# Moving two token-major product steps to the front of a layer's last eighth in a fused two-layer trunk

## The chip, the cores and the metric

The kernel runs on one core of a Trainium2 chip. The metric is the device time of one execution in microseconds (us); the median of several runs is compared. The core has a TensorE (PE in the profile, with its weight loads as PEld), a VectorE (DVE), a ScalarE (ACT), a GpSimd (POOL) and a SyncE (SP) whose queue issues most of the transfers here. Each engine works through its own list of instructions in order.

## The reference

Two decoder layers over 256 tokens of width 2048, in float32. Each layer is a mixing half and an MLP half, with a residual add behind each; one RMSNorm stands at the end.

```python
for l in range(2):
    h = rms_norm(x, norm1_g[l])
    q, k, v, gu, gv = split(h @ w_in[l])            # 2048 x 5120
    mix = concat(dilated_attention(rotary(q), rotary(k), v),
                 chunked_gmlp(gelu(gu), gelu(gv), ...))
    x = x + mix @ w_out[l]                           # 2048 x 2048
    h2 = rms_norm(x, norm2_g[l])
    x = x + square(relu(h2 @ w_up[l])) @ w_down[l]   # 2048 x 8192, 8192 x 2048
return rms_norm(x, final_g)
```

The change lies in the last line of a layer, in the second projection (`w_down`).

## The kernel before

**Number format.** Every float32 product is made of three products of a faster format. A weight tile `raw` (128 partitions x 1024 numbers, 512 KB) is loaded by SP (line 143); ScalarE writes its high part `hi` (line 152), VectorE the low part `lo`, the difference (line 162), called a lo plane below. TensorE then multiplies hi by the high part of the activations, lo by their high part and hi by their low part, and adds all three in one PSUM bank. The activations are split in the same way: `hs` holds the two parts of the gained x (lines 269 and 273), `half` those of the hidden values (lines 611 and 612).

**Steps.** All weight products stand in one list, `steps`. An entry is the weight tile or tiles it uses, a function `mm` that issues its matmuls, and a function that is called when a sum is complete. Most entries are feature-major steps (`transposed`, lines 380 to 384): one tile, 24 matmuls with 256 moving columns. A few are token-major steps (`fast`, lines 408 to 411): the first 512 output columns of `w_down` are made by a Winograd-like scheme with seven block products instead of eight. Such a step has four tile entries: `Top` and `Bottom`, which are loaded, and two `Sums`, which VectorE makes from them in place (lines 202 to 206) and which are then split like any tile. It has 42 matmuls. Two such steps (halves of a 1024-row piece) make one eighth of those columns.

**Eighths.** The MLP is cut in eighths of 1024 hidden columns. The loop runs e from 0 to 8: it puts the first projection of eighth e in the list (`up`, 16 steps), with the two token-major steps (`quick`) of eighth e - 1 put in among them, and behind them the feature-major steps of the second projection of eighth e - 1 (`down`, 12 steps, x chunks 4 to 15, two steps for a pair of chunks). The last round, e = 8, has no first projection, so its two token-major steps are put among the 12 steps of `down` instead. That round is called the last eighth below.

**Updates.** Behind each second step of a pair, `update(norm, c, ...)` adds the sum to two chunks of x (line 471, VectorE). In the last eighth the sum is final, and `update` also prepares the next norm: in the first layer it writes the chunks of `hs` for the next layer (lines 269 and 273) and adds their squares to `nacc` (lines 282 and 286); in the second layer, instead of `hs`, it scales x by the final gain (line 290). For the last pair of the second layer the two chunks are worked one by one (line 280).

**The queued work.** The token-major sums of all eighths stay in four `aux` PSUM banks. When the last is complete, `combine` (lines 744 to 751, ScalarE and VectorE) joins the seven products, two `turn_back`s (line 760, TensorE) bring them to feature-major form, and two `update`s add them to x chunks 0 to 3. These go through a queue written out by hand: `later(delay, cost, fn)` gives an item a due count, `run_queue` runs due items at the end of each step, up to a budget of 1.2 (the first item always runs). The count `now` is the number of tile entries used before the step: a feature-major step adds one, a token-major step four.

**Look-ahead.** In front of step n the program issues ScalarE's `hi` up to six tile entries ahead and VectorE's `lo` up to five, and loads as long as six `raw` buffers allow. There are 7 hi and 6 lo buffers. VectorE's instructions thus stand in one order: lo planes, updates, sums of tiles and combine, as the list gives them.

**The end of a layer.** Behind the first layer's last eighth the next layer begins: its first steps (`natural`, lines 431 to 433) read chunks 0 and 1 of `hs`, then 2 and 3, and so on. Behind the second layer's last eighth, `factor` sums the squares on TensorE (line 297: eight records on `nacc`, eight on the last pair's `nsq`), ScalarE takes a root (line 320), VectorE works on it, `spread` copies it to all partitions on TensorE (line 305), and nine products (line 876) with nine stores (line 877) end the kernel.

Of the kernel before, what the change touches and what calls it, by code (L numbers as in the profile page):

```python
# [83 lines left out]
def trunk(ctx: ExitStack, tc: tile.TileContext, layout, xT, consts, gains, w, b_sp, w_sp, out):  # L84
# [142 lines left out]
    def later(delay, cost, fn):  # L227

        queue.append((now[0] + delay, cost, fn))
# [115 lines left out]
    def collect(fn, *args, **kw):  # L345
        n = len(steps)
        fn(*args, **kw)
        part = steps[n:]
        del steps[n:]
        return part  # L350
# [92 lines left out]
    def from_tiles(tiles, n):  # L443
        return lambda k: tiles[k // n][0][:, k % n, :, :]
# [21 lines left out]
    def update(norm, c, ps, final, last):  # L466

        alone = last and final and c == KC - 2
        for j in range(2) if alone else [slice(0, 2)]:
            xj = x[:, c + j, :] if alone else x[:, c:c + 2, :]  # L470
            vec.tensor_tensor(xj, xj, ps[j][:, 0:S] if alone else pair(ps)[:, j, :], op=OP.add)  # L471
        if final:
            if not last:
                norm.chunks(c)
            norm.square(c, alone)
            if last:
                norm.gain(c)

    def layer(l, n1, n2, n3, last):
# [230 lines left out]
        def after_up(e):  # L710
            def f(c, ps):
                if hid[e][0] is None:
                    new_half(hid[e])
                z = inner[:, c // P:c // P + 2, :]
                vec.tensor_tensor(z, pair(ps), n2.R[:, None, :].to_broadcast([P, 2, S]), op=OP.mult)  # L715
                vec.scalar_tensor_tensor(z, z, 0.0, z, op0=OP.max, op1=OP.mult)  # L716
                to_half(hid[e][0], c // P, z)
                if c == 768:
                    summed[0] = False
                    if e == 0:  # L720
                        new_shared(F32R)
                        sum_parts[0] = shared[0].rearrange("p (k h t) -> p k h t", k=NH, h=2)
                    later(1, 1.5, sums)
            return f
# [40 lines left out]
        for e in range(9):  # L765
            up, down, quick = [], [], []
            if e < 8:
                up = collect(transposed, "w_up", l, 0, KC, e * 1024, 1024, from_hs, after_up(e))
            if e:
                down = collect(transposed, "w_down", l, (e - 1) * 1024, 8, FAST, D - FAST, from_tiles([hid[e - 1]], NH),  # L770
                               lambda c, ps, e=e: update(n3, (c + FAST) // P, ps, e == 8, last), apart=last and e == 8)
                quick = collect(fast, "w_down", l, (e - 1) * 1024, 0, [hid[e - 1]], banks, e == 1, e == 8,
                                lambda: later(1, 1.5, combine))
            rest = up or down
            at = (10, 11) if e == 1 else (6, 7)
            for i, one in enumerate(rest):
                if quick and i in at:
                    steps.append(quick.pop(0))
                steps.append(one)
            if up:  # L780
                steps.extend(down)
# [12 lines left out]
    for l in range(DEPTH):  # L794
        layer(l, norms[2 * l], norms[2 * l + 1], norms[2 * l + 2], l == DEPTH - 1)
# [118 lines left out]
```

## Time and profile before

| | |
|---|---|
| median of 3 runs | 2072.18 us (2071.5 to 2073.22) |
| profiled execution, own time | 2072.85 us |
| its span | 2071.1 us |
| busy: PE / DVE / ACT | 2046.6 / 1464.8 / 1010.8 us |
| granted TensorE clock, mean | 0.994 |
| DMA | 395.38 MB, mean 191 GB/s |

In the profile a line of the trace's order has a start in us from the span's start, a duration, an engine, a source line, an operation, its output and inputs, and in brackets the idle time in front of it with the instruction that ended it. A granted clock of 1.00 is full speed. Matmuls overlap: the record of one is 0.28 us, but one starts about every 0.11 us. The last eighth of the first layer begins at 979.32 us and that of the second at 2006.10 us.

### The profile page before, as it was taken

The page shows a single profiled execution, that of the slowest core. Times are in us where ns is not written, and L with a number is a line of the kernel's source. Part 1 is how long each engine was busy: PE and PEld are TensorE (multiplying, and loading weights), DVE is VectorE, ACT ScalarE, POOL GpSimd, SP SyncE. Part 2 cuts the span into 40 slices and gives each one's busy share as a digit, 9 for nine tenths or more (in the row PEclk, how much of TensorE's full clock was granted, in tenths as well). Part 3 has the DMA queues.
Part 4 walks back from the last instruction along what each step waited for, and adds up shares of the span by engine and source line. Part 5 has one row for each costly group of instructions (what it writes and reads, how often), then busy time and mean ns, then how long its engine had stood idle before and what let it go on. Part 6 is the DMA issues. An engine that isn't in the chain of part 4 may idle for free.

```text
span 2071.1 us, 40400 instructions
## 1 busy us (share of the span) xinstructions
PE 2046.6 (99%) x17066; PEld 2008.2 (97%) x17066; DVE 1464.8 (71%) x1800; ACT 1010.8 (49%) x1265; POOL 68.8 (3%) x90
## 2 busy tenths in 40 slices
PE   9999999999999999999899999999999999999996
PEld 8998999999999999999889989999999999999996
DVE  7666756777787677876855666668677776777766
ACT  7555444444454444544545654544454444544443
POOL 0002300000000000000000032000000000000000
PEclk9999999999999999999999999999999999999998
DMA  8555655576465655656554555555655655556552
GB/s 318 181 164 177 191 194 181 166 232 203 157 225 193 201 202 162 225 192 204 175 188 160 172 184 181 194 185 185 202 197 177 230 191 183 203 177 230 186 183 82
DMA packets 112118, 395.38 MB, mean 191 GB/s; under 512 B 12352, under 2 KB 16448, under 8 KB 111936
## 3 DMA queue, kind: packets, MB, share of 16 engines
q1 hardware_dynamic: 110800, 389.86, 56.6%
q8 instruction: 133, 2.18, 0.4%
q10 hardware_dynamic: 1136, 2.94, 0.4%
q14 instruction: 49, 0.40, 0.1%
HBM read 390.65 MB, written 2.10 MB: 190 GB/s over the span
## 4 chain that ended last, share of the span: by engine, by line
PE 96%; DVE 2%; ACT 1%; issue 0%; DMA 0%; ACTq 0%; DVEq 0%
PE acc L382 26%; PE acc L384 26%; PE acc L380 26%; PE acc L431 3%; PE acc L433 3%; PE acc L432 3%; PE aux L408 2%; PE aux L410 2%; PE aux L411 2%; DVE lo L162 1%; PE aux L657 0%; PE aux L559 0%; PE aux L601 0%; PE aux L297 0%; DVE x L471 0%
## 5 line engine op out<-in xcount | busy, mean ns | idle before, releaser
L152 ACT ACTIVATE hi<-raw 128x1024 fp32r<-128x1024 f32 (+1 forms) x773 | 785.1, 1047 | 404.4 <-PE acc L384 226.3
L162 DVE TENSOR_TENSOR lo<-raw,hi 128x1024 fp32r<-128x1024 f32 (+1 forms) x773 | 910.0, 1216 | 43.2 <-ACT hi L152 23.4
L380 PE MATMUL acc<-hs,hi 128*128 128x256 f32 x2816 | 780.5, 277 | 0.0
L384 PE MATMUL acc<-hs,hi 128*128 128x256 f32 x2816 | 778.0, 276 | 0.0
L382 PE MATMUL acc<-hs,lo 128*128 128x256 f32 x2816 | 778.0, 276 | 0.0
L380 PE MATMUL acc<-half,hi 128*128 128x256 f32 x2048 | 565.9, 276 | 0.0
L382 PE MATMUL acc<-half,lo 128*128 128x256 f32 x2048 | 565.5, 276 | 0.3 <-DVE lo L162 0.3
L384 PE MATMUL acc<-half,hi 128*128 128x256 f32 x2048 | 565.4, 276 | 0.0
L380 PEld LDWEIGHTS acc<-hs,hi 128*128 128x128 f32 x2816 | 529.1, 188 | 0.4 <-issue 0.2
L382 PEld LDWEIGHTS acc<-hs,lo 128*128 128x128 f32 x2816 | 528.8, 188 | 0.4 <-issue 0.2
L384 PEld LDWEIGHTS acc<-hs,hi 128*128 128x128 f32 x2816 | 528.6, 188 | 0.0
L382 PEld LDWEIGHTS acc<-half,lo 128*128 128x128 f32 x2048 | 384.5, 188 | 0.5 <-DVE lo L162 0.5
L380 PEld LDWEIGHTS acc<-half,hi 128*128 128x128 f32 x2048 | 384.5, 188 | 0.0
L384 PEld LDWEIGHTS acc<-half,hi 128*128 128x128 f32 x2048 | 384.5, 188 | 0.0
L471 DVE TENSOR_TENSOR x<-x,acc 128x512 f32<-128x512 f32 (+1 forms) x113 | 77.0, 681 | 170.4 <-PE acc L384 170.3
L611 ACT ACTIVATE half<-ar 128x512 fp32r<-128x512 f32 x72 | 45.6, 634 | 300.7 <-DVE ar L716 286.1
L715 DVE TENSOR_TENSOR ar<-acc,nR 128x512 f32<-128x512 f32 x64 | 44.3, 692 | 171.0 <-PE acc L384 170.9
L431 PE MATMUL acc<-hi,hs 128*128 128x512 f32 x256 | 102.8, 402 | 5.5 <-ACT hs L269 5.5
L433 PE MATMUL acc<-hi,hs 128*128 128x512 f32 x256 | 101.4, 396 | 0.0
L432 PE MATMUL acc<-lo,hs 128*128 128x512 f32 x256 | 101.1, 395 | 0.0
L612 DVE TENSOR_TENSOR half<-ar,half 128x512 fp32r<-128x512 f32 x72 | 49.8, 692 | 50.8 <-ACT half L611 50.8
L269 ACT ACTIVATE hs<-x,cols 128x256 fp32r<-128x256 f32 x64 | 29.0, 501 | 92.6 <-DVE x L471 91.4
(127 smaller groups left out, 1584.3 us busy)
## 6 DMA issues: line engine op xcount, KB each, us to landing
raw<-in_w SPq DMA_DIRECT2D x731, 512.0 KB, 4.5
raw<-in_w SPq DMA_DIRECT2D x10, 256.0 KB, 5.4
x<-in_xT SPq DMA_DIRECT2D x7, 256.0 KB, 5.7
out<-x SPq DMA_DIRECT2D x7, 256.0 KB, 3.1
shared<-in_b_sp ACTq DMA_DIRECT2D x2, 512.0 KB, 6.8
shared<-in_w_sp ACTq DMA_DIRECT2D x2, 512.0 KB, 8.2
con<-in_consts ACTq DMA_DIRECT2D x1, 512.0 KB, 7.5
x<-in_xT ACTq DMA_DIRECT2D x1, 256.0 KB, 4.2
```

Source lines behind the costliest of these rows:

```text
L152: act.activation(self.h[:, j * m:(j + 1) * m], self.raw[:, j * m:(j + 1) * m], AF.Copy)
L162: vec.tensor_tensor(lo[:, r], self.raw[:, r], self.h[:, r].bitcast(F32), op=OP.subtract)
L380: pe.matmul(o, lhsT=hi, rhs=xs[:, 0, :], start=(k0 + k == 0 and (two or cb == 0)), stop=False, skip_group_check=True)
L382: pe.matmul(o, lhsT=wt.lo[:, k, cb * P:(cb + 1) * P], rhs=xs[:, 0, :], start=False, stop=False, skip_group_check=True)
L384: pe.matmul(o, lhsT=hi, rhs=xs[:, 1, :], start=False, stop=last, skip_group_check=True)
L431: pe.matmul(ps, lhsT=xh, rhs=hi, start=(k0 + k == 0), stop=False)
L432: pe.matmul(ps, lhsT=xh, rhs=lo, start=False, stop=False)
L433: pe.matmul(ps, lhsT=xl, rhs=hi, start=False, stop=(k0 + k == KC - 1))
L471: vec.tensor_tensor(xj, xj, ps[j][:, 0:S] if alone else pair(ps)[:, j, :], op=OP.add)
L611: act.activation(t[:, c:c + 2, 0, :], src, AF.Copy)
L612: vec.tensor_tensor(t[:, c:c + 2, 1, :], src, t[:, c:c + 2, 0, :].bitcast(F32), op=OP.subtract)
L715: vec.tensor_tensor(z, pair(ps), n2.R[:, None, :].to_broadcast([P, 2, S]), op=OP.mult)
```

## The change

In the loop over eighths, `at` names the two places in the list at which the token-major steps are put in. For e = 8 it goes from (6, 7) to (0, 1): the order d0 to d5, q0, d6, q1, d7 to d11 becomes q0, d0, q1, d1, d2 to d11. The other eighths keep their places. It holds for both layers.

```diff
             rest = up or down
-            at = (10, 11) if e == 1 else (6, 7)
+            at = {1: (10, 11), 8: (0, 1)}.get(e, (6, 7))
             for i, one in enumerate(rest):
                 if quick and i in at:
                     steps.append(quick.pop(0))
                 steps.append(one)
```

## The prediction

> **What bounds the kernel now.** I read the page's head first, then the list of waits on TensorE, then the stretches of the two layer ends with their granted clock, then the order of instructions on TensorE, VectorE and ScalarE there. The head and the waits of PE (line waited for, total us, times, longest):
>
> ```profile
> span 2071.1 us, 40400 instructions
> PE 2046.6 (99%) x17066; PEld 2008.2 (97%) x17066; DVE 1464.8 (71%) x1800; ACT 1010.8 (49%) x1265; POOL 68.8 (3%) x90
> ...
> PE acc L431 <- ACT hs L269: 5.5, 2, 5.2
> PE aux L297 <- DVE nacc L286: 5.0, 1, 5.0
> PE aux L305 <- DVE nr L331: 1.2, 1, 1.2
> PE aux L760 <- DVE ar L750: 1.1, 2, 0.7
> PE aux L837 <- DVE warm L833: 1.1, 1, 1.1
> PE aux L410 <- DVE lo L162: 0.6, 1, 0.6
> PE acc L382 <- DVE lo L162: 0.3, 1, 0.3
> ```
>
> TensorE is the bound: busy 99% of the span. All its named waits are 14.8 us, and the two large ones are single events: one of 5.2 us in front of the next layer's first matmul (L431 waits for a chunk of hs), one of 5.0 us in front of the last normalisation's sums (L297 waits for nacc). Both follow a last eighth. A time can fall through TensorE's waits, or through the clock it gets. The stretches around those two waits (us; busy of PE, PEld, DVE, ACT, POOL; granted clock; DMA):
>
> ```profile
> 1025.10:1030.50 5.40, 0.16 (x2) 0.00 (x1) 4.21 (x8) 2.31 (x6) 0.00 (x0) 0.89 0.58 208
> 1030.50:1036.10 5.60, 5.60 (x13) 4.44 (x14) 4.95 (x9) 4.24 (x8) 0.86 (x1) 0.50 0.50 187
> 1036.10:1044.00 7.90, 7.90 (x36) 6.45 (x36) 5.54 (x3) 3.11 (x3) 2.18 (x1) 1.00 0.60 194
> ...
> 2050.30:2055.28 4.98, 0.00 (x0) 0.00 (x0) 3.00 (x5) 4.01 (x9) 0.00 (x0) 0.80 0.00 0
> 2055.28:2061.30 6.02, 4.79 (x20) 4.41 (x20) 0.72 (x5) 0.43 (x2) 0.00 (x0) 0.50 0.00 0
> ```
>
> After each wait the clock column reads 0.50: each wait is paid a second time, in matmuls at half speed. Where the idle stretch itself reads 0.89, the clock was full for 4.2 of its 5.40 us (x + 0.5(1 - x) = 0.89); with 0.80, for 3.0 of 4.98 us. Now TensorE in order: the last eighth of the first layer, the boundary, and the last eighth of the second layer (start, duration, what):
>
> ```profile
> 979.32 0.28 PE L380 MATMUL acc<-half,hi 128*128 128x256 f32 x1
> ...
> 1021.92 0.60 PE L760 MATMUL aux<-con,ar 128*128 128x128 f32 x4
> 1022.28 0.37 PE L380 MATMUL acc<-half,hi 128*128 128x256 f32 x1
> ...
> 1024.98 0.28 PE L384 MATMUL acc<-half,hi 128*128 128x256 f32 x1
> 1030.50 0.79 PE L431 MATMUL acc<-hi,hs 128*128 128x512 f32 x1 [5.24 <-ACT hs L269]
> ...
> 1036.16 0.39 PE L432 MATMUL acc<-lo,hs 128*128 128x512 f32 x1
> ...
> 2006.10 0.28 PE L380 MATMUL acc<-half,hi 128*128 128x256 f32 x1
> ...
> 2050.02 0.28 PE L384 MATMUL acc<-half,hi 128*128 128x256 f32 x1
> ```
>
> The eighth's twelve feature-major steps of 24 matmuls and two token-major steps of 42 are 372 matmuls between 979.32 and 1024.98; 2006.10 is the same place one layer later.
>
> **The change part by part.** Nothing is added or removed. The two token-major steps (call them q0 and q1) go from places 6 and 7 of the eighth to its front: q0, d0, q1, d1, d2 ... d11. With them move their four weight loads on SP's queue (SP issues only loads and, at the very end, output), their splits on ScalarE and VectorE, and all that is queued behind q1: combine, two turn_backs, and the updates of x chunks 0 and 2. POOL's queue is not passed: in this stretch it has only one product in the next layer's start.
>
> Where the queued work falls is counted from the code. The counter grows by 4 at a q step and by 1 at a d step; an item runs at the end of the first step whose counter, taken at that step's start, has reached it. Before: combine after d7, the turn_backs after d9 and d10, update(0) after d11, update(2) after the next layer's start. After: combine after d1, the turn_backs after d3 and d4, update(0) after d5, update(2) after d6. The last eighth then ends with update(14), whose hs chunks the next layer reads only in its eighth step, so the wait at L431 loses its cause. In the last layer nacc needs nothing after update(14), so the wait at L297 loses its cause too.
>
> First term, the first layer's eighth. For steps free of waits I take d0 to d5 as they ran before, in front of q0, and q0 itself:
>
> ```profile
> 995.64 0.28 PE L408 MATMUL aux<-hi,half 128*128 128x256 f32 x1
> ...
> 1000.40 0.28 PE L380 MATMUL acc<-half,hi 128*128 128x256 f32 x1
> ```
>
> 995.64 - 979.32 = 16.32 us for 144 matmuls is 0.1133, so 2.72 us a d step; q0 took 4.76. The eighth without waits is 12 x 2.72 + 2 x 4.76 + 2 x 0.36 (a turn_back, 1021.92 to 1022.28) = 42.9 us. It took 1030.50 - 979.32 = 51.2. Term: **-8.3 us** (5.4 of it the boundary, the rest the late lo planes at L382 and L410, the wait at L760, and their restarts).
>
> Second term, the slow clock behind the boundary: 13 matmuls from 1030.50 to 1036.16, 5.66 us (the count is in the stretch at clock 0.50); at the rate of the stretch behind (7.90 us for 36, 0.219) they take 2.9. Term: **-2.7 us**, if no new wait of 3 us or more stands there.
>
> Third, the last layer's eighth: 2050.02 + 0.11 - 2006.10 = 44.0 against 42.9. Term: **-1.1 us**.
>
> Fourth, the tail. The rows, and behind them the same two helpers earlier in the second layer, in dense work:
>
> ```profile
> 2050.79 0.42 ACT L280 ACTIVATE nsq<-x 128x256 f32<-128x256 f32 x1 [0.94 <-DVE x L471]
> 2051.11 0.89 ACT L290 ACTIVATE x<-x,cols 128x256 f32<-128x256 f32 x2
> ...
> 2055.28 1.86 PE L297 MATMUL aux<-ones,nacc 128*128 128x1 f32 x8 [4.99 <-DVE nacc L286]
> 2057.01 1.84 PE L297 MATMUL aux<-ones,nsq 128*128 128x1 f32 x8
> 2058.89 0.26 ACT L320 ACTIVATE nr<-aux,warm 128x2 f32<-128x2 f32 x1 [3.45 <-PE aux L297]
> 2060.06 1.22 PE L305 MATMUL aux<-con,nr 128*128 128x128 f32 x4 [1.21 <-DVE nr L331]
> ...
> 1364.61 0.95 PE L297 MATMUL aux<-ones,nacc 128*128 128x1 f32 x8
> 1368.32 0.61 PE L305 MATMUL aux<-con,nr 128*128 128x128 f32 x4
> ```
>
> After the change L297's first eight start right behind the last product (2050.1), at the full clock (0.95 for eight), the last four of the second eight wait for the square that ends at 2051.21, and all end near 2051.9. ScalarE is then just through with its two gains (2051.11 + 0.89 = 2052.0), and L320 starts there, not at 2058.89: 6.9 us. L305 takes 0.61 for 1.22 if the clock holds: 0.6. Term: **-7.5 us** (6.9 if the clock falls). The final products and the output behind it keep their order.
>
> Now the costs: who covers the moved work. VectorE is the engine that must. Its rows in the first layer's eighth:
>
> ```profile
> 979.52 0.69 DVE L471 TENSOR_TENSOR x<-x,acc 128x512 f32<-128x512 f32 x1 [2.48 <-PE acc L384]
> ...
> 1000.88 0.69 DVE L175 TENSOR_TENSOR lo<-raw,hi 128x512 fp32r<-128x512 f32 x1
> ...
> 1005.52 8.19 DVE L162 TENSOR_TENSOR lo<-raw,hi 128x1024 fp32r<-128x1024 f32 x7
> 1013.63 0.69 DVE L471 TENSOR_TENSOR x<-x,acc 128x512 f32<-128x512 f32 x1
> ...
> 1016.42 0.42 DVE L745 TENSOR_TENSOR ar<-ar,aux 128x256 f32<-128x256 f32 x1
> ...
> 1019.11 1.22 DVE L162 TENSOR_TENSOR lo<-raw,hi 128x1024 fp32r<-128x1024 f32 x1
> ```
>
> A lo plane costs 1.16 (1005.52 to 1013.63 for seven); a q's planes 4.64 (1000.88 to 1005.52) plus two planes, 7.0; a final update holds the engine 2.79 (1013.63 to 1016.42, ScalarE's part in its middle); combine 2.69 (to 1019.11). Set the eighth's start to zero. q0's planes must be made before it, in the last four d steps of the seventh eighth. These leave VectorE idle for 2.48 us once in two steps (the row at 979.52), and the time of four planes that they made before is free for q0's: 2 x 2.48 + 4 x 1.16 = 9.6 us for 7.0. Covered. Behind zero: the seventh's last add to x (0.24 to 0.85), d0's plane (2.0), q1's lump (9.0). TensorE asks for q1's last plane at 4.76 + 2.72 + 30 x 0.1133 = 10.9. Covered by 1.9. Then the planes of d1 to d5, to 14.8; d1's sums end at 15.0. From 15.2, in the queue's order, six updates (4, 6, 8, 0, 2, 10), combine, the planes of d6 to d11 and that of the next layer's first step: 16.7 + 2.7 + 8.1 = 27.5, done at 42.7. TensorE gets there at 42.9. Covered, by 0.2, and by 0.7 more since the first update starts nacc and adds nothing to it. The next layer's third step is the next narrow place: a plane, update(12) and a plane more, 42.7 + 5.1 = 47.8, against 42.9 + 24 x 0.219 = 48.2. So the cover is complete and thin; if it is gone, TensorE waits as long as VectorE slips. The last layer's update has no second part of hs, so its cover is thicker. SP's moved loads are priced by this row:
>
> ```profile
> raw<-in_w SPq DMA_DIRECT2D x731, 512.0 KB, 4.5
> ```
>
> A load waits for a plane some six tiles earlier, then lands in 4.5 us. The tightest is d5's: behind the third plane of q1 (7.8), landed at 12.3, wanted by VectorE at 13.6, which leaves 1.3 us for ScalarE's split. Covered too. Below nothing the cost of a thin cover can't go. I take 1.0 us for it, nearest to the 0.9 us that the same planes cost in all before (L410, L382), and 3 as the upper end (0.9 plus the 2 us by which one update more would pass all margins). ScalarE's moved work is on no path: 49% busy. The start's two loads for the next layer stand on ScalarE's queue behind update(14) as before, not behind update(0) too.
>
> Sum: -8.3 - 2.7 - 1.1 - 7.5 + 1.0 = **-18.6 us**. The profiled execution took 2072.85 (span 2071.1, 1.75 around it); the median of the runs is 2072.18, 0.67 lower. So 2054.3 for a profiled execution and **2053.6** for the median.
>
> The clock term against a rule: row first, 5.66 us at half clock behind a 5.24 us wait. The Trainium skill, TensorE: Matmul & The Clock Gate, section "What's actually happening", says that an idle window of about 3.4 us halves the clock and that a busy window of about 3.4 us gives it back, in windows that run freely. Estimate from that page: a single window at half clock costs 1.7 us, not 2.7, and the sum would be -17.6. The row is longer than one window, and I keep it.
>
> **The rivals.**
> One: VectorE slips past its thin cover by more than 3 us and TensorE waits that long for lo planes near the first layer's end. For it: the margins of 0.2 to 0.4 us just worked out; before, q1 already waited 0.6 at L410. Against: the seven earlier eighths pass the same planes with no wait in the list. Price, from 2072.2 - 19.6 = 2052.6 with no wait at all: 3 us in one piece still keep the clock (full for 3.0 and 4.2 us in the two idle stretches), 2055.6, the forecast's upper end; with 4 us it falls again, 4 + 2.7, 2059.3.
> Two: that wait grows to the old length and replaces it, slow clock included, so only the last layer gains: 2072.2 - 1.1 - 7.5 = 2063.6. It needs VectorE 5 us later than the ledger.
> Three, slower: q0 and q1 at the front find no planes. Place: the step from the seventh eighth to q0, because one step now takes four entries of a look-ahead counted in tiles. Price: the lump of 7.0 uncovered and the clock's 2.7 behind it, at two q's in two layers, 38.8 against a gain of 19.6: 2091. It decides once the four waits, with the clock, pass 4.9 us each. Against: the 9.6 us for 7.0 above, and the waits on planes before, 0.9 us over 32 such steps.
> Four: the change does nothing, because the queued work still lands behind d11: 2072.2. Against: the count of places above.
>
> **How the numbers follow.** Forecast 0.72 (2051 to 2056), rival one 0.16, two 0.06, four 0.02, three 0.04. The forecast's low end is 2052.6, no wait at all, less the 1.7 us over which the runs shown spread (2071.5 to 2073.22); the range goes through rival one, its 2059.3 and the same 1.7: 2051 to 2061, leaving out two, three and four, 0.12. What this kernel's timing can tell from no change is about 0.2%, 4 us. Faster 0.94 (forecast, one, two), same 0.02, slower 0.04.
>
> **What would show it.** Right: no wait of L431 on hs and none of L297 on nacc over 0.5 us; clock 1.00 through the first layer's end; L320 about 2 us after the last L384; L745 some 18 us after the eighth's start. Wrong: a wait of L431 or L380 on lo (rival one or two), of L408 to L411 on lo or hi at the eighth's front (three), or L745 where it was (four).

## The result, and the profile after

The median went from 2072.47 to 2054.53 us (four runs each; 2054.42 to 2054.67 after), a ratio of 0.9914 with a 95% interval of 0.9897 to 0.9931: 17.9 us less, 0.9%. The forecast was 2053.6. The profiled execution took 2054.54 us, its span is 2052.8, 18.3 less than before.

The head of the page and the whole list of TensorE's waits in the changed kernel:

```profile
span 2052.8 us, 40389 instructions
PE 2040.6 (99%) x17066; PEld 2004.3 (98%) x17066; DVE 1464.6 (71%) x1800; ACT 1009.3 (49%) x1265; POOL 68.0 (3%) x90
...
PE aux L305 <- DVE nr L331: 1.2, 1, 1.2
PE aux L837 <- DVE warm L833: 1.1, 1, 1.1
PE acc L431 <- ACT hs L269: 0.2, 1, 0.2
```

Before, 14.8 us of waits were named; now it is 2.5. The two of 5 us are gone, and so are those on lo planes and on combine; the 0.2 of L431 lies at the kernel's start, where each kernel here has 0 to 0.8 of it. VectorE and ScalarE did the same work in nearly the same busy time (1464.8 and 1010.8 us before). The stretches that answer to those of before (the first layer's last eighth, the next layer's start, the tail; same columns):

```profile
979.51:1022.90 43.39, 43.39 (x382) 43.39 (x381) 38.23 (x53) 25.45 (x36) 0.00 (x0) 1.00 0.55 188
1022.90:1030.50 7.60, 7.60 (x36) 6.25 (x35) 6.37 (x11) 4.89 (x9) 0.00 (x0) 1.00 0.68 219
...
2039.20:2043.60 4.40, 2.56 (x22) 2.28 (x20) 1.73 (x8) 1.48 (x4) 0.00 (x0) 1.00 0.00 0
```

TensorE is busy for all of the 43.39 us, and the clock column, which read 0.89 and then 0.50 at these places, reads 1.00 three times. In order of time on TensorE, with q1's first product and the one behind q1, the boundary, and the tail:

```profile
987.10 0.28 PE L408 MATMUL aux<-hi,half 128*128 128x256 f32 x1
...
992.05 0.28 PE L380 MATMUL acc<-half,hi 128*128 128x256 f32 x1
...
1022.79 0.28 PE L384 MATMUL acc<-half,hi 128*128 128x256 f32 x1
1022.90 0.39 PE L431 MATMUL acc<-hi,hs 128*128 128x512 f32 x1
1023.13 0.39 PE L432 MATMUL acc<-lo,hs 128*128 128x512 f32 x1
...
2039.09 0.28 PE L384 MATMUL acc<-half,hi 128*128 128x256 f32 x1
2039.21 0.95 PE L297 MATMUL aux<-ones,nacc 128*128 128x1 f32 x8
2040.02 1.03 PE L297 MATMUL aux<-ones,nsq 128*128 128x1 f32 x8
2042.26 0.71 PE L305 MATMUL aux<-con,nr 128*128 128x128 f32 x4 [1.21 <-DVE nr L331]
```

The next layer's first product follows the eighth's last by 0.11 us, where 5.52 lay between them; the natural products stand 0.23 us apart from the first on. L297 follows its last product by 0.12 us, where it was 5.26. ScalarE at the end:

```profile
2040.19 0.89 ACT L290 ACTIVATE x<-x,cols 128x256 f32<-128x256 f32 x2
2041.09 0.26 ACT L320 ACTIVATE nr<-aux,warm 128x2 f32<-128x2 f32 x1
```

L320 now starts 2.00 us after the last product (8.87 before), right behind the two gains.

VectorE in the first layer's eighth, two rows of the ledger: the start of combine, and the planes of the next layer's first two steps:

```profile
997.44 0.42 DVE L745 TENSOR_TENSOR ar<-ar,aux 128x256 f32<-128x256 f32 x1 [0.30 <-ACT ar L744]
...
1020.90 2.35 DVE L162 TENSOR_TENSOR lo<-raw,hi 128x1024 fp32r<-128x1024 f32 x2
```

The first of the two planes at 1020.90 is the one that decides whether the boundary has a wait. At 1.22 us it is done at 1022.12; L432, which reads it, starts at 1023.13. So the cover held, by 1.0 us.

### The profile page after: what moved, and what is told of

It reads as the page before. It is cut to its first block, busy times and chain, and to the rows that moved or that the text cites. A ratio compares the mean times of both kernels' runs of the same rounds, so it can differ in the third digit from the quotient of the medians.

```text
span 2052.8 us, 40389 instructions
## 1 busy us (share of the span) xinstructions
PE 2040.6 (99%) x17066; PEld 2004.3 (98%) x17066; DVE 1464.6 (71%) x1800; ACT 1009.3 (49%) x1265; POOL 68.0 (3%) x90
## 4 chain that ended last, share of the span: by engine, by line
PE 99%; DVE 0%; DMA 0%; ACT 0%; ACTq 0%; issue 0%; DVEq 0%
PE acc L384 27%; PE acc L382 27%; PE acc L380 27%; PE acc L431 3%; PE acc L433 3%; PE acc L432 3%; PE aux L408 3%; PE aux L411 3%; PE aux L410 3%; PE aux L657 0%; PE aux L601 0%; PE aux L559 0%; PE aux L588 0%; DVE x L876 0%; DMA x<-in_xT 0%; PE aux L562 0%
## 5 line engine op out<-in xcount | busy, mean ns | idle before, releaser
L382 PE MATMUL acc<-hs,lo 128*128 128x256 f32 x2816 | 779.1, 277 | 0.0
L382 PE MATMUL acc<-half,lo 128*128 128x256 f32 x2048 | 566.1, 276 | 0.0
L382 PEld LDWEIGHTS acc<-hs,lo 128*128 128x128 f32 x2816 | 528.9, 188 | 0.4 <-issue 0.2
L382 PEld LDWEIGHTS acc<-half,lo 128*128 128x128 f32 x2048 | 384.6, 188 | 0.0
L431 PE MATMUL acc<-hi,hs 128*128 128x512 f32 x256 | 101.7, 397 | 0.2 <-ACT hs L269 0.2
L433 PE MATMUL acc<-hi,hs 128*128 128x512 f32 x256 | 100.7, 393 | 0.0
L432 PE MATMUL acc<-lo,hs 128*128 128x512 f32 x256 | 100.0, 391 | 0.0
L612 DVE TENSOR_TENSOR half<-ar,half 128x512 fp32r<-128x512 f32 x72 | 49.9, 693 | 50.6 <-ACT half L611 50.6
```

What stands on the lines that cost most here:

```text
L382: pe.matmul(o, lhsT=wt.lo[:, k, cb * P:(cb + 1) * P], rhs=xs[:, 0, :], start=False, stop=False, skip_group_check=True)
L431: pe.matmul(ps, lhsT=xh, rhs=hi, start=(k0 + k == 0), stop=False)
L432: pe.matmul(ps, lhsT=xh, rhs=lo, start=False, stop=False)
L433: pe.matmul(ps, lhsT=xl, rhs=hi, start=False, stop=(k0 + k == KC - 1))
```

## The experiments

All ratios are to the kernel before, with 95% intervals. Two theories stood at the start: that the two updates behind the eighth's end were what TensorE waited for, at two places, each wait paid again in clock; and, against it, that the place of the steps works by giving VectorE room for their planes.

**The first layer alone, and the second alone.**

```diff
-at = {1: (10, 11), 8: (0, 1)}.get(e, (6, 7))
+at = {1: (10, 11), 8: (6, 7) if last else (0, 1)}.get(e, (6, 7))   # first alone
+at = {1: (10, 11), 8: (0, 1) if last else (6, 7)}.get(e, (6, 7))   # second alone
```

> The two steps stand at the front in the first layer's last eighth only; the second layer's is as before. Theory (the two late updates each leave one wait, in two places that have nothing to do with each other): the first layer's eighth and boundary lose 7.8 us and the slow clock behind it 2.7 us, so about 2062.0 us, with the wait of L297 on nacc still 5.0 us. Rival (the gain is one effect, a VectorE that runs ahead from the first layer on): most of the 18 us are there already, about 2056 us, and the wait of L297 shrinks too.

> The two steps stand at the front in the second layer's last eighth only. Theory: the eighth loses 0.6 us and the tail 7.4 us, so about 2064.5 us, with the wait of L431 on hs still 5.2 us and half clock behind it. With the kernel of the first layer alone the two gains add up to the whole, 18 us within 1 us. Rival (one effect from the first layer on): under 3 us of gain, 2069.5 us or more.

Measured: 2062.28 us (ratio 0.9951, 0.9936 to 0.9965) and 2064.76 us (0.9962, 0.9947 to 0.9977), against 2072.56 before. The gains of 10.3 and 7.8 add up to 18.1; both together gave 17.9. In the waits of each, the other layer's wait is whole. First alone, then second alone:

```profile
PE aux L297 <- DVE nacc L286: 5.0, 1, 5.0
...
PE acc L431 <- ACT hs L269: 5.3, 2, 5.2
```

So they are two effects at two places, and the one-effect rival falls.

**Filling the two waits with idle products.** It separates a wait from the slow clock behind it, with no wait of the real work taken away.

```diff
+def fill(n):
+    ps = acc_bank()
+    for _ in range(n):
+        pe.matmul(ps[:, 0:P], lhsT=ones, rhs=ones, start=True, stop=True)
...
         if l:
+            mark(lambda: fill(26))
             mark(start)
...
     n = norms[-1]
+    fill(24)
     n.factor(warm[:, 1:2])
```

> The kernel before with idle TensorE kept at work: 26 products of a constant tile with itself in front of the second layer's start and 24 in front of the last sums of squares, into a free bank that nobody reads. No wait of the real work is taken away. Theory (each wait is paid a second time at half clock): the first natural products take 0.23 us apart, not 0.43, and L297's sixteen records 1.8 us, not 3.6, and L305 0.7, not 1.2: 2.7 + 1.7 + 0.5 = 4.9 us less, 2067.5 us. Rival (the slow matmuls come from cold operands or from the wait itself and not from idleness): same as before, 2072.4 us.

Measured: 2068.81 us (0.9981, 0.9971 to 0.9990), 3.75 us less. The stretch that read 0.50 before, and the sums of the tail (five more source lines stand ahead of them here: L302 is L297, and L436 to L438 are L431 to L433). The rows between show the first natural product and the fourteenth:

```profile
1030.50:1036.10 5.60, 5.60 (x30) 4.73 (x29) 4.69 (x8) 4.24 (x8) 0.00 (x0) 1.00 0.27 93
...
1031.11 0.47 PE L436 MATMUL acc<-hi,hs 128*128 128x512 f32 x1
...
1034.17 0.39 PE L437 MATMUL acc<-lo,hs 128*128 128x512 f32 x1
...
2053.40 0.95 PE L302 MATMUL aux<-ones,nacc 128*128 128x1 f32 x8
2054.22 1.03 PE L302 MATMUL aux<-ones,nsq 128*128 128x1 f32 x8
```

The first 13 natural products took 3.06 us instead of 5.66 (of the 30 records in the stretch 8 are idle products), and sixteen sums 1.85 us instead of 3.57: the slow clock is a cost of its own, and idleness is its cause. The 4.9 expected was not reached. An idle product took 0.22 us, so the 26 ran some 0.3 us past the end of the wait, and the 24 in the tail 0.2. That is about half of the 1.15 us that are missing; the rest stays open.

**An earlier queue, the steps left at places 6 and 7.**

```diff
-lambda: later(1, 1.5, combine))
+lambda: later(0, 1.5, combine))
...
-later(2, 1.5, lambda: turn_back(0, c11, c21))
-later(2, 1.5, lambda: turn_back(2, c12, c22))
+later(0, 1.5, lambda: turn_back(0, c11, c21))
+later(0, 1.5, lambda: turn_back(2, c12, c22))
```

> The two steps stay at places 6 and 7, but combine and the two turn_backs are queued without delay, so that the updates of chunks 0 to 3 come before the last update instead of behind it. Theory (it is the late updates that TensorE waits for, and the place of the steps matters because it sets how early the queue runs): the tail's 7.4 us go wholly; at the first layer's boundary VectorE is still in arrears with the planes, so the wait on hs falls to about 3 us in two pieces, the clock stays full: 5 to 6 us there; together 2059 to 2060.5 us. Rival (the place itself matters, since the q steps' planes crowd the middle): no more than 3 us of gain, 2069 us or more.

Measured: 2060.35 us (0.9942, 0.9927 to 0.9956), a total as the theory gave. Its parts are a little off: the tail gave 6.4 us of its 7.4 (11.3 to 4.9), the first layer 6.3 where 5 to 6 were expected. Two thirds of the gain (12.2 of 18 us) come with no step moved, only by bringing the updates ahead of the last one. What is left in the waits:

```profile
PE acc L431 <- ACT hs L269: 2.3, 3, 0.8
...
PE aux L410 <- DVE lo L162: 0.7, 1, 0.7
PE aux L297 <- DVE nacc L286: 0.7, 1, 0.7
```

No wait among these is longer than 0.8 us, and the clock held (one of L431's three, 0.7, is at the kernel's start). What is left is VectorE in arrears: late hs chunks, late planes and late squares. The waits on them, with one of 0.3 us on a plane at L382, make 3.3 of the 5.8 us that this kernel lacks to the change; the other 2.5 lie for the most part in shorter gaps between products that the list does not name.

**Other places.**

```diff
-at = {1: (10, 11), 8: (0, 1)}.get(e, (6, 7))
+at = {1: (10, 11), 8: (4, 5)}.get(e, (6, 7))   # and, in another kernel, 8: (2, 3)
```

> The two steps stand at places 4 and 5 of the last eighth in both layers, two steps earlier than before and four later than at the front. The queue then runs update(0) behind d9 and update(2) behind d10, both before the last update. Theory (what counts is that the updates come before the last one, and VectorE's whole work in the eighth is the same): nearly the whole gain, 2054.5 to 2056.5 us, with at most 1 us of waits on planes or hs in the first layer. Rival (only the front gives VectorE the room): waits of 3 us or more at the first layer's end, 2058 us or more.

> The two steps stand at places 2 and 3 of the last eighth. Theory: as at the front, 2054.5 us within 1 us, no wait over 0.5 us. Rival (only the front gives VectorE the room): between the front and places 4 and 5.

Measured: 2059.31 us at places 4 and 5 (0.9934, 0.9917 to 0.9950), 2055.09 us at 2 and 3 (0.9914, 0.9894 to 0.9934). The second is as the theory gave. The first missed the theory's upper end by 2.8 us: the rival, that the place itself gives VectorE room, has its share, though the waits of 3 us or more that it named did not come. The waits at places 4 and 5, and L305's products in their tail:

```profile
PE acc L431 <- ACT hs L269: 0.8, 1, 0.8
PE aux L760 <- DVE ar L750: 0.7, 1, 0.7
PE aux L297 <- DVE nacc L286: 0.7, 1, 0.7
PE aux L410 <- DVE lo L162: 0.4, 1, 0.4
...
2046.94 1.22 PE L305 MATMUL aux<-con,nr 128*128 128x128 f32 x4 [1.21 <-DVE nr L331]
```

L305's four records took 1.22 us here and 0.71 in the change: the clock fell at about 2044.9, in the midst of the sums of L297, with no wait in this tail longer than 0.7 us until then. So a short wait does not always keep the clock; the slow clock cost about 0.5 us at L305. Why it fell here stays open.

Where the room lies is seen in VectorE's idle time ahead of the eighth. The seventh's last two adds and the eighth's last update, first at the front, then at places 2 and 3, then at 4 and 5:

```profile
974.27 0.69 DVE L471 TENSOR_TENSOR x<-x,acc 128x512 f32<-128x512 f32 x1 [1.56 <-PE acc L384]
979.71 0.69 DVE L471 TENSOR_TENSOR x<-x,acc 128x512 f32<-128x512 f32 x1 [0.99 <-PE acc L384]
1028.23 0.68 DVE L471 TENSOR_TENSOR x<-x,acc 128x512 f32<-128x512 f32 x1
```

```profile
974.19 0.69 DVE L471 TENSOR_TENSOR x<-x,acc 128x512 f32<-128x512 f32 x1 [2.48 <-PE acc L384]
979.63 0.69 DVE L471 TENSOR_TENSOR x<-x,acc 128x512 f32<-128x512 f32 x1 [1.56 <-PE acc L384]
1029.52 0.68 DVE L471 TENSOR_TENSOR x<-x,acc 128x512 f32<-128x512 f32 x1
```

```profile
974.41 0.69 DVE L471 TENSOR_TENSOR x<-x,acc 128x512 f32<-128x512 f32 x1 [2.48 <-PE acc L384]
979.85 0.69 DVE L471 TENSOR_TENSOR x<-x,acc 128x512 f32<-128x512 f32 x1 [2.48 <-PE acc L384]
1031.24 0.68 DVE L471 TENSOR_TENSOR x<-x,acc 128x512 f32<-128x512 f32 x1
```

The bracket is idle time that VectorE could not use. It is 2.55 us in the two gaps at the front, 4.04 at places 2 and 3, 4.96 at 4 and 5. The look-ahead is counted in tile entries: four entries ahead of the eighth's start are q0's, worth 7.0 us of VectorE, or four plain planes, worth 4.6. What isn't made there is missing at the end: from the seventh's last add to update(14) it is 48.5 us at the front, 49.9 and 51.4 at the other places, and VectorE is busy for 42.9, 44.2 and 45.1 of them.

**Places 4 and 5 with the earlier queue.** If VectorE's arrears are set by the place, the order of its work can't take them away.

```diff
+at = {1: (10, 11), 8: (4, 5)}.get(e, (6, 7))
+# combine and both turn_backs with later(0, ...), as above
```

> Places 4 and 5 with combine and the turn_backs queued without delay, so that update(0) and update(2) stand behind d7 and d8. Theory now (at places 4 and 5 VectorE itself is 2 to 3 us later at the first layer's end, since it could make less of the two steps' planes in the idle time ahead of the eighth; the order of its work only says who waits): the waits on hs go, waits on planes take their place, 2 to 3 us in the first layer; the second layer's tail gets its 1.5 us back; 2057 to 2058.5 us. Rival (at places 4 and 5 it was only update(2) behind d10 that came too late): no waits in the first layer either, 2054.5 to 2055.5 us.

Measured: 2056.96 us (0.9924, 0.9908 to 0.9941; 2056.3 to 2057.9), at the theory's lower edge. Its list of waits on TensorE, and VectorE from the seventh's last add to update(14):

```profile
PE aux L410 <- DVE lo L162: 0.4, 1, 0.4
PE acc L432 <- DVE lo L162: 0.4, 1, 0.4
...
980.45 0.69 DVE L471 TENSOR_TENSOR x<-x,acc 128x512 f32<-128x512 f32 x1 [2.48 <-PE acc L384]
...
1031.94 0.68 DVE L471 TENSOR_TENSOR x<-x,acc 128x512 f32<-128x512 f32 x1
```

The arrears are the same, 51.5 us, and the waits went from hs to planes, but they are smaller than the 2 to 3 us expected. Of the 4.8 us that places 4 and 5 lose to the front, the earlier queue won back 2.35 and 2.4 are left. Both theories hold a part; neither alone explains this kernel. The parts do not simply add up: at the front the earlier queue costs time, as the next kernel shows, and against that one this kernel is only 1.1 us slower. About 0.5 us here is again L305 at half clock (1.23 us).

Two pairs of these kernels have update(0) and update(2) behind the same steps and differ in the place, and with it in where combine stands. Behind d7 and d8, places 2 and 3 took 2055.09 us and places 4 and 5 with the earlier queue 2056.96; behind d9 and d10, places 4 and 5 took 2059.31 and places 6 and 7 with the earlier queue 2060.35. So two places further to the front went with 1 to 2 us less, though the two updates stayed where they were.

**The front with the earlier queue.** A try at a version that beats both.

> The changed kernel with combine and the turn_backs queued without delay. Theory (in the changed kernel TensorE waits for nothing in either eighth, so an earlier queue has nothing to win): 2054.5 us within 0.7 us. Rival (the earlier queue puts combine ahead of planes that the thin cover needs): new waits on planes in the first layer, 2055.5 us or more.

Measured: 2055.86 us (0.9920, 0.9905 to 0.9935), 1.3 us over the change alone, outside the 0.7 allowed, and slower as the rival said (2055.39 to 2056.41 in four runs, against 2054.42 to 2054.67). VectorE's start of combine and the planes behind it, then TensorE behind the first turn_back:

```profile
991.82 0.42 DVE L745 TENSOR_TENSOR ar<-ar,aux 128x256 f32<-128x256 f32 x1 [1.86 <-PE aux L411]
...
994.51 2.35 DVE L162 TENSOR_TENSOR lo<-raw,hi 128x1024 fp32r<-128x1024 f32 x2
...
995.79 0.39 PE L382 MATMUL acc<-half,lo 128*128 128x256 f32 x1
```

Combine now stands ahead of four planes and waits 1.86 us for q1's end, with the planes behind it. The first of them ends at 995.73, and L382, which reads it, starts at 995.79, 0.44 us behind the product before it, where 0.11 is usual. The list of waits does not name this gap; the times show it. The same gap lies in the second layer. The two are about half of the 1.3 us; where the rest goes stays open. So no version here beats the change.

**How thin the cover is.** VectorE gets additions that nobody needs, behind update(2) in the first layer's last eighth of the changed kernel: four in one kernel, eight in the other.

```diff
-later(0, 1.5, lambda: update(n3, c, ps, True, last))
+later(0, 1.5, lambda: (update(n3, c, ps, True, last), pad() if c == 2 and not last else None))
...
+def pad():
+    for _ in range(4):   # 8 in the other
+        vec.tensor_tensor(blocks[:, 0:2, :], blocks[:, 0:2, :], blocks[:, 2:4, :], op=OP.add)
```

> The changed kernel with four VectorE additions of 128x512 (0.7 us each, 2.8 us together) that nobody needs, behind update(2) in the first layer's last eighth. Theory of the thin cover (in the changed kernel the plane of the next layer's first step is ready 0.9 to 1.0 us before TensorE asks for it): TensorE waits for planes for 1.8 to 2.0 us in all, the clock stays full, so 2056.4 us. Rival (the cover is thicker, since hs and planes have room that the order does not show): no wait, 2054.5 us.

> The same with eight such additions, 5.6 us. Theory: waits of 4.6 to 4.8 us in all, in two or three pieces of which the largest is about 3.6 us; if that piece is long enough for the clock to fall, 2 to 3 us more: 2059.2 us with a full clock, 2062 us with a half one. Rival (thicker cover): under 3 us of wait, 2057 us or less.

Measured: 2056.88 us (0.9923, 0.9903 to 0.9943) and 2059.87 us (0.9937, 0.9917 to 0.9957), 2.35 and 5.3 us over the change (two runs each; with eight they took 2059.10 and 2060.64). With four, then with eight, and then the stretch of the longest wait with the one behind it:

```profile
PE acc L432 <- DVE lo L162: 0.8, 1, 0.8
...
PE acc L382 <- DVE lo L162: 0.6, 1, 0.6
```

```profile
PE acc L382 <- DVE lo L162: 3.5, 1, 3.5
...
PE acc L432 <- DVE lo L162: 0.8, 1, 0.8
...
1019.90:1023.60 3.70, 0.24 (x4) 0.04 (x2) 3.60 (x6) 0.00 (x0) 0.00 (x0) 1.00 0.00 0
1023.60:1026.30 2.70, 2.70 (x23) 2.70 (x24) 2.08 (x5) 2.14 (x4) 0.00 (x0) 1.00 0.58 184
```

The waits on planes are 1.4 us for 2.8 us of additions and 4.3 us for 5.6, so 1.3 to 1.4 us were hidden, where I had 0.9 to 1.0; behind that TensorE loses about a microsecond for a microsecond, as rival one priced it. The times lost a little more than the waits: 2.35 us with four and, in the profiled execution, 4.6 with eight. A wait of 3.5 us in one piece left the clock at 1.00.

## Why the prediction was right

The terms, as measured between the same rows:

| term | forecast | measured | from |
|---|---|---|---|
| first layer's last eighth and boundary | -8.3 | -7.8 | 51.2 to 43.4 us |
| slow clock behind the boundary | -2.7 | -2.7 | 48 natural products: 13.7 to 11.0 us |
| second layer's last eighth | -1.1 | -0.6 | 44.0 to 43.4 us |
| tail, last product to first L876 | -7.5 | -7.4 | 11.3 to 3.9 us |
| thin cover | +1.0 | 0 | no wait on planes |
| sum | -18.6 | -18.5 | span -18.3 |

The mechanism came out step by step: combine 17.9 us after the eighth's start (18 said), update(2) before the last update, no wait on hs or on nacc, full clock, L320 2.0 us behind the last product.

Two steps were mis-sized, and they cancel; that the sum of the terms came out within 0.1 us is luck. "The eighth without waits is ... 42.9 us" is half a microsecond too low, twice. I had q0's 4.76 us for both token-major steps, but q1 takes 4.95 (987.10 to 992.05), and the feature-major steps run a little over 2.72. "I take 1.0 us for it", the price of the thin cover, should have been nothing: the ledger's own result, 42.7 less 0.7 against 42.9, was near the measured one (the plane done at 42.6, wanted at 43.6), and I added a price out of caution.

Rivals one and two did not come; the additions to VectorE show that one's mechanism is real and starts 1.3 to 1.4 us further on. For rival three, the row at 979.71 shows VectorE still idle for 0.99 us in front of the eighth's start: q0's planes were made in the idle time of the seventh, as the 9.6 us for 7.0 said. What I had not seen is that this is a benefit of the front and not only a cost that it avoids. The forecast's argument by due counts alone would have given places 4 and 5 the same gain, and there it fails by 4.8 us, of which about half came back with the earlier queue.

The rule on the clock: 13 slow products took 5.66 us before, and the measured term of 2.7 us agrees with that row. For losing the clock there are several rows: the wait of 3.46 us kept it, the idle stretches at the two layer ends were 4.2 and 3.0 us old when it fell, and in the tail at places 4 and 5 it fell with no wait longer than 0.7 us before it. The Trainium skill, TensorE: Matmul & The Clock Gate, section "What's actually happening", gives a window of about 3.4 us for losing the clock and for gaining it, and says that it runs freely. By a single window the change would have gained about 1 us less than the forecast's sum, an estimate from that page. The 4.2 and the 3.46 us agree with such a window; the 3.0 us and the fall at places 4 and 5 came sooner than one whole idle window, and there the measurement decides.

## What to carry to other kernels

Where TensorE is busy 99% of the span, look for the single long waits at the seams between stages, and price those of the length seen here (5 us) twice: the wait and the half clock behind it. One of 3.5 us was paid once. Work that the next stage needs first should be queued so that it ends ahead of the seam; when a step is moved, count where each thing queued behind it will run. A look-ahead counted in entries makes a step with costly preparation cheap just behind a stage in which the preparing engine idles, and dear where that engine is already full.

## What the runs showed of the hardware that was not expected

With TensorE some 8 us earlier at the boundary and free of its wait, VectorE's small norm chain starts at 1035.56 us instead of 1045.16, and GpSimd's mask product of the next layer, which waits for a load, fell together with it. Two rows of the changed kernel:

```profile
1036.74 2.31 DVE L329 SCALAR_TENSOR_TENSOR rt<-nr 128x2 f32<-128x2 f32 x1
...
1036.63 2.40 POOL L492 TENSOR_TENSOR shared<-shared,con 128x1024 f32<-128x1024 f32 x1 [808.01 <-DMA shared<-in_w_sp]
```

The same VectorE instruction on 128x2 numbers takes 0.16 us elsewhere; here it lasted until 1039.05, GpSimd until 1039.03. The Trainium skill, SBUF — State Buffer, section "Who interferes with whom", says that a VectorE instruction with two SBUF inputs contends with a GpSimd instruction that reads SBUF, since its second input uses the shared read interface. The rows agree. Before the change the same product (3.05 us) ran beside four lo planes, which took 6.84 us there and take 4.62 in the changed kernel. TensorE did not wait for it here.
